# Forming the right operands of a seven-product stage in the tiles of the product before it

## The chip, the cores and the metric

The kernel runs on one core of a Trainium2 chip. The metric is the device time of one execution in microseconds; a comparison is made between medians of several runs. The engines are TensorE (PE; its weight loads are listed as PEld), VectorE (DVE), ScalarE (ACT), GpSimd (POOL) and SyncE (SP), which here only issues DMAs. Times inside an execution are counted from the start of its span.

## What is computed

One transformer-like block over 2048 tokens of width 1024, all in float32: an RMS norm and one input projection, stick-breaking attention (8 heads) beside a gated spatial mixing, an output projection with the residual, and then the part that this change is about:

```
h   = rmsnorm(x, norm_mlp_g)
act = square(relu(h @ w_up))        # 1024 -> 4096
x   = x + act @ w_down              # 4096 -> 1024
out = rmsnorm(x, norm_final_g)
```

## The kernel before, in words

The tokens are worked on in four chunks `c` of 512. Each float32 product is made of three matmuls (`mm3`, L87): an operand is split by `split` (L78) into a high half, which ScalarE rounds (L81), and a low half, which VectorE takes as the difference (L82), and the matmuls are high x high (L89), high x low (L90) and low x high (L91).

The stages that matter stand at the end of the program. Chunks 0 and 1 go through the feed-forward part by plain products: `up_plain` (L592) and `down_plain` (L615). `down_plain` runs over eight groups `g` of the inner width and, in each, over four turns: a chunk (left operand, from `act_d`) times a half of the output columns (right operand, from `w_down`). Chunk and half alternate so that each operand serves two turns, and in the last group the second and the fourth turn also finish a chunk: `finish` (L668) norms each block of 128 rows and stores it through POOL's queue.

Chunks 2 and 3 together go through the feed-forward part by Strassen's method in Winograd's form, with seven products where eight would be needed. `up_seven` (L730) runs over 16 steps `q` of the inner width. In each q it makes seven products of twelve matmuls, in the order 0, 4, 5, 6, 1, 3, 2 (`ORDER`, L417). The right operands, the same for all q, come from the two chunks' `h`: four blocks are loaded from DRAM into tiles `w8` (`Rights`, L675), operand 0 is split at once into its own tiles `x8` (L685), and `rest` (L698) forms the other six as pairs of tiles (high and low) of 8 KB per partition each, and two halves of a subtraction (L703). The left operands are formed per q from a block of `w_up` (`Lefts`, L710) with additions on POOL (L719, L746, L748, L753); their tiles come from the same `w8`. The seven results are combined on VectorE (L770 to L788), squared after relu on ScalarE, and combined once more by `keep_acts` (L579; L582 to L585), which stores seven planes to `s_d` with one DMA per q (L586). `down_seven` (L812) reads these planes back and makes the seven products with `w_down`; its first group needs the tile `new` (L837), which POOL writes (L847).

Tiles come from pools. A pool has so many tiles under a name, and a new tile of that name waits until one is free again, that is until all its users are done, DMAs too. `Room` (L424) holds the names: `t8` are tiles of 8 KB per partition, `t4` of 4 KB. Up to the end of `down_plain` the pool `mp` (L974) has 14 `t8`, two `t4` and the tile `gmlp_t`. Then it is closed (`low.close()`, L1009), and the pool `mlp` (L1012) is laid over its memory, with 12 `t8`, two `acts` of 14 KB and two `t2`. `Rights` and the first `Lefts` are traced before the end of `down_plain` (L1006, L1007), since their tiles lie in the pool `hx` elsewhere, but `rest`, which needs `t8`, is called from within `up_seven` at q = 0 (L736, L751, L756).

The order of each engine's instructions is made by the tile framework when the program is built: it takes them in the order of the source, moved by a model of when each is ready. `together` (L916) interleaves two generators in the source: so many steps of `side` for each step of `main`.

Of the kernel before, what the change touches and what calls it, by code (L numbers as in the profile page):

```python
# [8 lines left out]
F32 = mybir.dt.float32  # L9
F32R = mybir.dt.float32r  # L10
BF16 = mybir.dt.bfloat16
AF = mybir.ActivationFunctionType
ALU = mybir.AluOpType
PSUM = bass.MemoryType.PSUM
DRAM = bass.MemoryType.DRAM

P = 128
D = 1024
# [16 lines left out]
def block_kernel(ctx: ExitStack, tc: tile.TileContext, x, x_t, gmix, w_in, ln_g, ln_b, sgw, sgb,  # L35
# [542 lines left out]

    def keep_acts(q, acts):  # L579

        a11, a12, a21, a22, s1, s2, s4 = (acts[:, i] for i in (0, 1, 6, 3, 4, 5, 2))
        nc.vector.tensor_tensor(s1, a21, a22, ALU.add)  # L582
        nc.vector.tensor_tensor(s2, s1, a11, ALU.subtract)
        nc.vector.tensor_tensor(a21, a11, a21, ALU.subtract)
        nc.vector.tensor_tensor(s4, a12, s2, ALU.subtract)  # L585
        nc.sync.dma_start(s_d[q // 4][:, :, q % 4, :].rearrange("i p t -> p i t"), acts)  # L586

# [26 lines left out]

    def down_plain(rm):  # L615

# [24 lines left out]
        for g in range(ND):  # L641
            lefts, rights = {}, {}
            for turn in range(4):
# [7 lines left out]
                if n not in rights:  # L651
                    rights[n] = right(n, g)
                a, b = lefts[c], rights[n]
                ns = slice(n * 512, (n + 1) * 512)
# [20 lines left out]
    class Rights:  # L675
# [21 lines left out]

        def rest(self, step):  # L698
            if step == 0:
                self.keep(4, self.b11)  # L700
                self.keep(5, self.t2)
                self.keep(1, self.b21)
                self.minus(self.b21, self.b21, self.t2)  # L703
            elif step == 1:
                self.keep(6, self.b12)
            else:
                self.keep(3, self.b21)
                self.keep(2, self.b22)

# [20 lines left out]
    def up_seven(rights, rm, ahead, before_last):  # L730
        hc = rights.hc
        for q in range(16):
            l = ahead if q == 0 else Lefts(rm, q)
            s12, a11, a12, a21, a22, w0, w4 = l.s, l.a11, l.a12, l.a21, l.a22, l.w0, l.w4
            if q == 0:
                rights.rest(0)  # L736

# [11 lines left out]
            w6 = l.operand(a21)  # L749
            if q == 0:  # L750
                rights.rest(1)  # L751
            w1 = l.operand(a12)
            nc.gpsimd.tensor_tensor(a12, a12, s12, ALU.subtract)  # L753
            w3 = l.operand(a22)
            if q == 0:
                rights.rest(2)  # L756
            w2 = l.operand(a12)
            acts = rm.get("acts", [7, TC])
            c11, c21, c22, c12 = acts[:, 0, :], acts[:, 1, :], acts[:, 3, :], acts[:, 6, :]
            u2, u3 = rm.get("t2", [TC]), c22  # L760
            b1 = rm.ps()
# [27 lines left out]
            relu2(c12, c12)  # L789
            keep_acts(q, acts)  # L790
            yield
# [20 lines left out]
    def down_seven(loads, rm):  # L812
# [19 lines left out]
        for g in range(NG):  # L832
# [3 lines left out]
            bs = loads.bs  # L836
            new = rm.get("acts", [2, 2, 512])  # L837

# [15 lines left out]
            for n, i in enumerate(ORDER_D):  # L854
                st = rm.raw8([4, TC])
                nc.sync.dma_start(st, s_d[g][i])
                key = {0: 1, 1: 1, 5: 6, 6: 7, 3: 7, 4: 5, 2: 5}[i]
# [16 lines left out]
                def done(tb):  # L874
# [8 lines left out]
                    elif i == 1:  # L883
                        into(ys[0][tb][:, lo], ps[tb])
                    elif i == 6:
                        into(acc[1][:, tb, :], ps[tb], g == 0)
                    elif i == 4:
                        into(acc[1][:, tb, :], ps[tb])
                        if last_g:
                            plus(ys[1][tb][:, hi], acc[1][:, tb, :])  # L890
                    elif i == 3:
                        into(ys[1][tb][:, lo], ps[tb])
                        if last_g:
                            finish(rm, rm.get("t2", [D], BF16), 3, tb, ys[1][tb], nc.sync)
                    else:
                        into(ys[0][tb][:, hi], ps[tb])
                        if last_g:
                            finish(rm, rm.get("t2", [D], BF16), 2, tb, ys[0][tb], nc.sync)

# [56 lines left out]
    with ExitStack() as es:  # L956
# [15 lines left out]
        gfin_t = gains.tile([P, D], F32, name="gfin_t")  # L972
        low = ExitStack()
        mp = low.enter_context(tc.tile_pool(name="mp", bufs=1, reuse_waits="tile"))  # L974
        gmlp_t = mp.tile([P, D], F32, name="gmlp_t")
        nc.sync.dma_start(gmlp_t, gmlp.broadcast_to([P, D]))
        nc.sync.dma_start(gfin_t, gfin.broadcast_to([P, D]))
        rm = Room(mp, ps_mm, dict(t8=N8, t4=2))
        hTs = []
# [14 lines left out]
        together(o.turn(), side, R_U)  # L994
        down = down_plain(rm)
        assert together(down, side, R_U) is OPEN
    with tc.tile_pool(name="ext", bufs=1, side="right", reuse_waits="tile") as ext, \
# [3 lines left out]
        for part in (o.operands, o.product, o.turn):  # L1001
            together(part(), down, 0.8)
    hx = ctx.enter_context(tc.tile_pool(name="hx", bufs=1, side="right", reuse_waits="tile"))
    rm = Room(None, None, dict(w8=5, raw8=2, x8=2, s12=1, t8=12, acts=2, t2=2),
              dict(w8=hx, raw8=hx, x8=hx, s12=hx))
    rights = Rights(rm)  # L1006
    ahead = Lefts(rm, 0)  # L1007
    together(down)
    low.close()  # L1009
    mm_stack.close()  # L1010
    with tc.tile_pool(name="ps_b", bufs=8, space=PSUM, reuse_waits="tile") as ps_b, \
            tc.tile_pool(name="mlp", bufs=1, reuse_waits="tile") as mlp:  # L1012
        rm.pool, rm.psum = mlp, ps_b
        loads = Down(rm)
        together(up_seven(rights, rm, ahead, lambda: loads.load(0)))
        together(down_seven(loads, rm))
# [38 lines left out]
```

## Time and profile before

| | us |
|---|---|
| median of 3 runs | 2518.61 (2518.34 to 2525.99) |
| the profiled execution's own time | 2518.97 |
| its span | 2517.2 |
| TensorE busy | 2430.1 (97%) |
| VectorE busy | 1694.0 (67%) |
| ScalarE busy | 1145.2 (45%) |
| POOL busy | 309.8 (12%) |

A matmul's record is longer than the distance to the next one, since matmuls are pipelined; what counts is from start to start. In a row of the timeline the bracket tells how long the engine was idle before it, and whom it waited for.

### The profile page before, as it was taken

Reading aid. Unit: us, or ns where it says so; the run is one execution under the profiler, and the core shown is the slowest. Engines: PE = TensorE matmul, PEld = TensorE weight load, DVE = VectorE, ACT = ScalarE, POOL = GpSimd, SP = SyncE. Lnnn points to the kernel's source line nnn. Section 1 sums busy time; section 2 is a strip of 40 time slices with the busy share of each in tenths; the row PEclk is TensorE's granted clock in tenths of the full one; section 3 lists DMA queues with packets and bytes.
Section 4 is the critical chain, followed back from the end, with each engine's and each line's share of the span. In section 5 each row is a group of like instructions: output and inputs, shape, how many; then the busy total and the mean of one; then the engine's idle time right before and its main releaser. Section 6 shows DMA issues by size and latency. Waiting matters only on the chain.

```text
span 2517.2 us, 30341 instructions
## 1 busy us (share of the span) xinstructions
PE 2430.1 (97%) x11424; PEld 1991.5 (79%) x11424; DVE 1694.0 (67%) x2280; ACT 1145.2 (45%) x2004; POOL 309.8 (12%) x255
## 2 busy tenths in 40 slices
PE   8999999997899999999999899999989999999998
PEld 7887788876677888888877688888867888778886
DVE  4643678877767666666668878644667556677788
ACT  5422446445536555555555534322244444433333
POOL 1100011000000000000000000000113322314432
PEclk9999999997999999999989999999999999999999
DMA  9747977679544343433364533343523434753422
GB/s 378 265 141 240 333 260 243 214 211 330 173 164 150 121 126 120 123 115 117 126 255 162 181 130 117 112 182 134 216 85 137 156 141 153 281 218 120 167 101 101
DMA packets 158226, 446.59 MB, mean 177 GB/s; under 512 B 12544, under 2 KB 28928, under 8 KB 138624
## 3 DMA queue, kind: packets, MB, share of 16 engines
q1 hardware_dynamic: 149744, 417.39, 48.5%
q0 software_dynamic: 4032, 25.17, 2.4%
q10 hardware_dynamic: 4304, 2.10, 0.3%
q8 instruction: 90, 1.47, 0.2%
q14 instruction: 56, 0.46, 0.1%
HBM read 314.59 MB, written 130.02 MB: 177 GB/s over the span
## 4 chain that ended last, share of the span: by engine, by line
PE 86%; DVE 8%; issue 3%; DMA 3%; ACT 1%; POOL 0%; POOLq 0%; SPq 0%; DVEq 0%; ACTq 0%
PE mm L91 24%; PE mm L90 24%; PE mm L89 23%; PE tr L370 4%; PE av L389 2%; PE z L346 2%; PE av L388 2%; PE z L345 2%; DVE w L82 2%; DVE t L82 1%; DVE pr L359 1%; PE mm L498 1%; DVE aT L82 1%; PE mm L263 1%; DMA t<-b_d 1%
## 5 line engine op out<-in xcount | busy, mean ns | idle before, releaser
L89 PE MATMUL mm<-t,t 128*128 128x512 f32 x1280 | 503.5, 395 | 0.4 <-DVE t L82 0.4
L91 PE MATMUL mm<-t,t 128*128 128x512 f32 x1280 | 503.5, 393 | 0.0
L90 PE MATMUL mm<-t,t 128*128 128x512 f32 x1280 | 502.3, 393 | 0.0
L359 DVE TENSOR_TENSOR_SCAN pr<-kk,pr,zeros 128x513 f32<-128x513 f32 x192 | 246.3, 1284 | 119.5 <-ACT kk L351 119.0
L351 ACT ACTIVATE kk<-z 128x512 f32<-128x512 f32 (+2 forms) x320 | 172.3, 538 | 296.3 <-PE z L346 158.7
L89 PEld LDWEIGHTS mm<-t,t 128*128 128x128 f32 x1280 | 242.4, 189 | 51.2 <-DVE t L82 0.8
L91 PEld LDWEIGHTS mm<-t,t 128*128 128x128 f32 x1280 | 241.8, 189 | 52.0
L90 PEld LDWEIGHTS mm<-t,t 128*128 128x128 f32 x1280 | 242.1, 189 | 50.0
L81 ACT ACTIVATE aT<-tr 128x512 fp32r<-128x512 f32 (+1 forms) x320 | 173.7, 545 | 107.6 <-PE tr L370 105.9
L82 DVE TENSOR_TENSOR aT<-tr,aT 128x512 fp32r<-128x512 f32 (+1 forms) x320 | 191.1, 598 | 21.6 <-ACT aT L81 21.3
L370 PE MATMUL tr<-ident,b 128*128 128x128 f32 x1088 | 180.9, 279 | 21.9 <-DVE aT L82 17.8
L90 PE MATMUL mm<-w,w 128*128 128x512 f32 x448 | 176.4, 394 | 8.8 <-DVE w L82 8.6
L81 ACT ACTIVATE t<-t 128x1024 fp32r<-128x1024 f32 x104 | 104.7, 1060 | 172.7 <-DMA t<-in_w_down 110.8
L370 PEld LDWEIGHTS tr<-ident,b 128*128 128x128 f32 x1088 | 133.0, 143 | 58.4 <-DVE aT L82 26.6
L91 PE MATMUL mm<-w,w 128*128 128x512 f32 x448 | 175.6, 392 | 0.0
L353 ACT ACTIVATE b<-z 128x512 f32<-128x512 f32 (+2 forms) x320 | 172.1, 539 | 2.6 <-PE tr L370 2.6
L356 DVE TENSOR_TENSOR_SCAN pr<-kk,zeros 128x128 f32<-128x128 f32 (+3 forms) x128 | 104.5, 820 | 96.9 <-ACT kk L351 96.7
L81 ACT ACTIVATE w<-raw 128x512 fp32r<-128x512 f32 (+1 forms) x135 | 106.4, 801 | 132.3 <-PE mm L91 119.9
L91 PE MATMUL mm<-t,w 128*128 128x512 f32 x380 | 150.4, 396 | 2.8 <-DVE w L82 2.8
L82 DVE TENSOR_TENSOR w<-raw,w 128x512 fp32r<-128x512 f32 (+1 forms) x135 | 149.0, 1106 | 3.4 <-ACT w L81 2.9
L90 PE MATMUL mm<-t,w 128*128 128x512 f32 x380 | 149.1, 393 | 1.4 <-DVE t L82 1.4
L82 DVE TENSOR_TENSOR t<-t,t 128x1024 fp32r<-128x1024 f32 x104 | 123.6, 1225 | 39.1 <-ACT t L81 19.4
(214 smaller groups left out, 4765.5 us busy)
## 6 DMA issues: line engine op xcount, KB each, us to landing
w_in<-wi_d SPq DMA_DIRECT2D x40, 1024.0 KB, 8.4
kt<-k_d SPq DMA_DIRECT2D x160, 256.0 KB, 4.9
t<-in_w_down SPq DMA_DIRECT2D x28, 1024.0 KB, 5.1
s_d<-acts SPq DMA_DIRECT2D x16, 1792.0 KB, 6.2
raw<-s_d SPq DMA_DIRECT2D x28, 1024.0 KB, 4.8
t<-wo_d SPq DMA_DIRECT2D x24, 1024.0 KB, 6.9
wi_d<-w_in POOLq DMA_DIRECT2D x20, 1024.0 KB, 9.5
vt<-v_d SPq DMA_DIRECT2D x80, 256.0 KB, 2.7
```

The costliest lines, as they stand in the source:

```text
L81: nc.scalar.activation(hi, src, AF.Copy)
L82: nc.vector.tensor_tensor(lo, src, hi.bitcast(F32), ALU.subtract)
L89: nc.tensor.matmul(ps, lh, rh, start=first, stop=False, skip_group_check=more)
L90: nc.tensor.matmul(ps, lh, rl, start=False, stop=False, skip_group_check=more)
L91: nc.tensor.matmul(ps, ll, rh, start=False, stop=last, skip_group_check=more)
L345: nc.tensor.matmul(z[:, :Z], ql, kt[:, 0, :Z], start=True, stop=False)
L346: nc.tensor.matmul(z[:, :Z], ql, kt[:, 1, :Z], start=False, stop=not diag)
L351: nc.scalar.activation(kk[:, :L], z[:, :L], AF.Sigmoid, scale=-QK_SCALE)
L353: nc.scalar.activation(b[:, :L], z[:, :L], AF.Sigmoid, scale=QK_SCALE)
L356: nc.vector.tensor_tensor_scan(pr[:, L - 1::-1], kk[:, L - 1::-1], zeros[:, :L], 1.0, ALU.mult, ALU.add)
L359: nc.vector.tensor_tensor_scan(pr[:, ::-1], kk[:, ::-1], zeros, carry[tb], ALU.mult, ALU.add)
L370: nc.tensor.transpose(tr[:, tb * P:(tb + 1) * P], bs[tb][:, j * P:(j + 1) * P], ident)
```

## The change

The pool `mp` is not closed any more; it stays to the end and serves the seven-product stages too, with 14 `t8` and three `t4`, one of which first holds `gmlp_t`. `rest` becomes a generator, and it is interleaved with the last two turns of `down_plain`, one step of it for every two steps of the product. The tile `acts` of seven planes is replaced by a `t8` of four planes, a `t4` with s1 and s2, and half of a `t4` with s4, whose other half is u2; so the store of a q becomes three DMAs, and the planes stand in another order in `s_d` (`PLACE`). `new` becomes a `t8`.

```
+    PLACE = (0, 1, 6, 3, 4, 5, 2)
+
+    def keep_acts(q, acts, s12, s4):
+
+        a11, a12, a21, a22 = (acts[:, i] for i in range(4))
+        s1, s2 = s12[:, 0], s12[:, 1]
         nc.vector.tensor_tensor(s1, a21, a22, ALU.add)
         nc.vector.tensor_tensor(s2, s1, a11, ALU.subtract)
         nc.vector.tensor_tensor(a21, a11, a21, ALU.subtract)
         nc.vector.tensor_tensor(s4, a12, s2, ALU.subtract)
-        nc.sync.dma_start(s_d[q // 4][:, :, q % 4, :].rearrange("i p t -> p i t"), acts)
+        dst = s_d[q // 4]
+        nc.sync.dma_start(dst[0:4, :, q % 4, :].rearrange("i p t -> p i t"), acts)
+        nc.sync.dma_start(dst[4:6, :, q % 4, :].rearrange("i p t -> p i t"), s12)
+        nc.sync.dma_start(dst[6, :, q % 4, :], s4)
...
-    def down_plain(rm):
+    def down_plain(rm, placed):
...
+                if g == ND - 1 and turn == 2:
+                    placed.append(True)
...
-        def rest(self, step):
...
+        def rest(self):
+            self.keep(4, self.b11)
+            yield
+            self.keep(5, self.t2)
+            yield
+            self.keep(1, self.b21)
+            yield
+            self.minus(self.b21, self.b21, self.t2)
+            self.keep(6, self.b12)
+            yield
+            self.keep(3, self.b21)
+            yield
+            self.keep(2, self.b22)
...
-            acts = rm.get("acts", [7, TC])
-            c11, c21, c22, c12 = acts[:, 0, :], acts[:, 1, :], acts[:, 3, :], acts[:, 6, :]
-            u2, u3 = rm.get("t2", [TC]), c22
+            acts, both = rm.t8([4, TC]), rm.t4([2, TC])
+
+            c11, c21, c12, c22 = (acts[:, i, :] for i in range(4))
+            u2, u3 = both[:, 0, :], c22
...
-            keep_acts(q, acts)
+            keep_acts(q, acts, rm.t4([2, TC]), both[:, 1, :])
...
-            new = rm.get("acts", [2, 2, 512])
+            new = rm.t8([2, 2, 512])
...
-                nc.sync.dma_start(st, s_d[g][i])
+                nc.sync.dma_start(st, s_d[g][PLACE[i]])
...
-                            finish(rm, rm.get("t2", [D], BF16), 3, tb, ys[1][tb], nc.sync)
+                            finish(rm, rm.t4([D], BF16), 3, tb, ys[1][tb], nc.sync)
...
-        low = ExitStack()
-        mp = low.enter_context(tc.tile_pool(name="mp", bufs=1, reuse_waits="tile"))
-        gmlp_t = mp.tile([P, D], F32, name="gmlp_t")
+        placed = []
+        mp = ctx.enter_context(tc.tile_pool(name="mp", bufs=1, reuse_waits="tile"))
+        rm = Room(mp, ps_mm, dict(t8=N8, t4=3))
+        gmlp_t = rm.t4([D])
...
-    rm = Room(None, None, dict(w8=5, raw8=2, x8=2, s12=1, t8=12, acts=2, t2=2),
-              dict(w8=hx, raw8=hx, x8=hx, s12=hx))
+    rm = Room(mp, ps_mm, dict(w8=5, raw8=2, x8=2, s12=1, t8=N8, t4=3), dict(w8=hx, raw8=hx, x8=hx, s12=hx))
     rights = Rights(rm)
     ahead = Lefts(rm, 0)
-    together(down)
-    low.close()
+    while not placed:
+        next(down)
+    rest = rights.rest()
+    if together(down, rest, 0.5) is OPEN:
+        together(down)
+    for _ in rest:
+        pass
     mm_stack.close()
-    with tc.tile_pool(name="ps_b", bufs=8, space=PSUM, reuse_waits="tile") as ps_b, \
-            tc.tile_pool(name="mlp", bufs=1, reuse_waits="tile") as mlp:
-        rm.pool, rm.psum = mlp, ps_b
+    with tc.tile_pool(name="ps_b", bufs=8, space=PSUM, reuse_waits="tile") as ps_b:
+        rm.psum = ps_b
```

The calls of `rest` inside `up_seven` are gone.

## Rows read from the trace of the kernel before

**Rows 1.** The page's busy time by engine, over the whole span.

```profile
PE 2430.1 (97%) x11424; PEld 1991.5 (79%) x11424; DVE 1694.0 (67%) x2280; ACT 1145.2 (45%) x2004; POOL 309.8 (12%) x255
```

**Rows 2.** TensorE by stretch: length, PE busy (matmuls), granted clock, DMA share, GB/s.

```profile
1780.00:1864.90 84.90, 84.90 (x376) 1.00 0.30 116
1864.90:1925.00 60.10, 49.62 (x195) 0.91 0.35 127
1925.00:2150.00 225.00, 225.00 (x984) 1.00 0.41 150
```

**Rows 3.** TensorE's timeline after the plain down product: start, length, line, matmul, idle before.

```profile
1869.89 0.50 PE L89 MATMUL mm<-t,raw 128*128 128x512 f32 x1 [2.03 <-ACT t L81]
1874.56 0.79 PE L90 MATMUL mm<-t,raw 128*128 128x512 f32 x1 [4.17 <-DVE t L82]
...
1879.42 0.58 PE L89 MATMUL mm<-t,w 128*128 128x512 f32 x1
...
1880.84 0.50 PE L91 MATMUL mm<-t,w 128*128 128x512 f32 x1 [0.37 <-DVE w L82]
...
1884.84 0.50 PE L90 MATMUL mm<-t,w 128*128 128x512 f32 x1 [1.43 <-DVE t L82]
...
1890.58 0.79 PE L91 MATMUL mm<-t,w 128*128 128x512 f32 x1 [2.48 <-DVE w L82]
...
1893.62 0.40 PE L89 MATMUL mm<-t,w 128*128 128x512 f32 x1
```

**Rows 4.** ScalarE's, VectorE's and POOL's timelines around the end of the plain down product.

```profile
1868.78 2.01 ACT L81 ACTIVATE t<-w 128x1024 fp32r<-128x1024 f32 x2 [1.68 <-DMA out_y<-t]
...
1868.64 1.28 DVE L672 SCALAR_TENSOR_TENSOR t<-t,nf_r,gfin_t 128x1024 f32<-128x1024 f32 x1 [1.36 <-POOL nf_r L75]
1873.28 6.90 DVE L82 TENSOR_TENSOR t<-w,t 128x1024 fp32r<-128x1024 f32 x6 [3.35 <-DMA out_y<-t]
...
1848.55 0.57 POOL L673 DMA_DIRECT2D out_y<-t  x1 [1.62 <-DVE t L672]
```

**Rows 5.** A stretch near that end: length, then PE, PEld, DVE, ACT, POOL busy.

```profile
1846.00:1865.00 19.00, 19.00 (x86) 15.73 (x85) 9.02 (x13) 3.45 (x6) 3.50 (x7) 1.00 0.20 84
```

**Rows 6.** SyncE's and VectorE's timelines in the first three q.

```profile
1879.65 25.83 SPq L716 DMA_DIRECT2D raw<-in_w_up  x3
1910.93 0.37 SPq L586 DMA_DIRECT2D s_d<-acts  x1
...
1924.73 1.03 DVE L582 TENSOR_TENSOR acts<-acts 128x512 f32<-128x512 f32 x1 [0.89 <-ACT acts L590]
...
1938.39 0.69 DVE L782 TENSOR_TENSOR acts<-mm,t 128x512 f32<-128x512 f32 x1 [4.68 <-PE mm L91]
```

**Rows 7.** DMA issues: queue, count, KB each, median us from issue to landing.

```profile
s_d<-acts SPq DMA_DIRECT2D x16, 1792.0 KB, 6.2
...
raw<-in_w_up SPq DMA_DIRECT2D x16, 1024.0 KB, 4.8
...
b_d<-u SPq DMA_DIRECT2D x16, 256.0 KB, 4.0
...
out_y<-t POOLq DMA_DIRECT2D x8, 512.0 KB, 2.9
```

**Rows 8.** Timelines where the down stage begins; last, the landing of L586's store at 2178.

```profile
2206.01 0.79 PE L90 MATMUL mm<-w,w 128*128 128x512 f32 x1 [5.34 <-DVE w L82]
...
2193.89 2.57 DVE L582 TENSOR_TENSOR acts<-acts 128x512 f32<-128x512 f32 x1 [0.23 <-ACT acts L590]
...
2204.74 1.21 DVE L82 TENSOR_TENSOR w<-acts,w 128x1024 fp32r<-128x1024 f32 x1
...
2192.61 3.30 POOL L847 TENSOR_TENSOR acts<-t,t 128x1024 f32<-128x1024 f32 x1 [1.77 <-issue]
...
2178.14 1.16 SPq L586 DMA_DIRECT2D s_d<-acts  x1
...
DMA to landing us min/median/max: 14.4/14.4/14.4
```

More of the change, by code (lines that the diff above doesn't have):

```diff
@@ L576, in turn @@
                     nc.sync.dma_start(h_d[self.c - 2][kk], self.hT[kk])
-    def keep_acts(q, acts):
-        a11, a12, a21, a22, s1, s2, s4 = (acts[:, i] for i in (0, 1, 6, 3, 4, 5, 2))
+    PLACE = (0, 1, 6, 3, 4, 5, 2)
+    def keep_acts(q, acts, s12, s4):
+        a11, a12, a21, a22 = (acts[:, i] for i in range(4))
+        s1, s2 = s12[:, 0], s12[:, 1]
         nc.vector.tensor_tensor(s1, a21, a22, ALU.add)
@@ L696, in keep @@
             split4(t, src)
-        def rest(self, step):
[L699 to L708, printed above, removed]
+        def rest(self):
[11 more added lines that the diff above has]
+            self.keep(2, self.b22)
     class Lefts:
@@ L734, in up_seven @@
             s12, a11, a12, a21, a22, w0, w4 = l.s, l.a11, l.a12, l.a21, l.a22, l.w0, l.w4
-            if q == 0:
-                rights.rest(0)
             def form(w, i, ps, first):
@@ L749, in up_seven @@
             w6 = l.operand(a21)
-            if q == 0:
-                rights.rest(1)
             w1 = l.operand(a12)
@@ L754, in up_seven @@
             w3 = l.operand(a22)
-            if q == 0:
-                rights.rest(2)
             w2 = l.operand(a12)
-            acts = rm.get("acts", [7, TC])
-            c11, c21, c22, c12 = acts[:, 0, :], acts[:, 1, :], acts[:, 3, :], acts[:, 6, :]
-            u2, u3 = rm.get("t2", [TC]), c22
+            acts, both = rm.t8([4, TC]), rm.t4([2, TC])
+            c11, c21, c12, c22 = (acts[:, i, :] for i in range(4))
+            u2, u3 = both[:, 0, :], c22
             b1 = rm.ps()
@@ L897, in done @@
                         if last_g:
-                            finish(rm, rm.get("t2", [D], BF16), 2, tb, ys[0][tb], nc.sync)
+                            finish(rm, rm.t4([D], BF16), 2, tb, ys[0][tb], nc.sync)
                 if last_g and n >= 5:
@@ L972, in block_kernel @@
         gfin_t = gains.tile([P, D], F32, name="gfin_t")
-        low = ExitStack()
-        mp = low.enter_context(tc.tile_pool(name="mp", bufs=1, reuse_waits="tile"))
-        gmlp_t = mp.tile([P, D], F32, name="gmlp_t")
+        placed = []
+        mp = ctx.enter_context(tc.tile_pool(name="mp", bufs=1, reuse_waits="tile"))
+        rm = Room(mp, ps_mm, dict(t8=N8, t4=3))
+        gmlp_t = rm.t4([D])
         nc.sync.dma_start(gmlp_t, gmlp.broadcast_to([P, D]))
         nc.sync.dma_start(gfin_t, gfin.broadcast_to([P, D]))
-        rm = Room(mp, ps_mm, dict(t8=N8, t4=2))
         hTs = []
@@ L994, in block_kernel @@
         together(o.turn(), side, R_U)
-        down = down_plain(rm)
+        down = down_plain(rm, placed)
         assert together(down, side, R_U) is OPEN
```

## The prediction

> **What bounds the kernel now.** I read the busy shares first: TensorE is busy 97% of the span and VectorE, next, 67% [rows 1], so time can only be won where TensorE is not fed at full speed. The busy time by stretch shows where that is [rows 2]. From 1780 to 1864.9 us, the end of the plain down product, TensorE has no idle time at a granted clock of 1.00. From 1864.9 to 1925, the first q of the seven-product stage, it is busy 49.6 of 60.1 us and the mean clock is 0.91. From 1925 to 2150 it is full again: 984 matmuls in 225 us, one per 0.2287 us.
>
> TensorE's timeline of the first dip names the waits [rows 3]. The twelve matmuls of product 0 follow the plain down product without a pause, since its right operand lies in its own tiles. Then TensorE waits 2.03 us for ScalarE's high half of right operand 4, 4.17 us for VectorE's low half, and 0.37, 1.43 and 2.48 us for further halves: 10.48 us. After two of these waits the matmuls start 0.43 us apart, the lower of the clock's two levels: 12 starts from 1874.56 to 1879.42 (11 intervals, 4.86 us where 11 x 0.2287 = 2.52 would do) and 8 from 1890.58 to 1893.62 (7 intervals, 3.04 instead of 1.60). That is 2.34 + 1.44 = 3.78 us more.
>
> The ScalarE, VectorE and POOL timelines say why the halves are late [rows 4]. The first ScalarE split of operand 4 waits for the landing of an output row block and starts at 1868.78; six VectorE splits (6.90 us, 1.15 us each) start at 1873.28, after waiting for the last of those blocks. The pool for these operands lies over the old pool's memory, so its tiles come free only as the plain product's last rows leave.
>
> **The change part by part.** *Right operands in the old pool's tiles.* The six operand pairs (4, 5, 1, 6, 3, 2) take 12 of the 14 tiles of the pool that now stays open. During the last two turns of the plain product (third and fourth of g = 7) ten are held: 4 by the results, 2 by the left pair, 4 by the two right pairs. So four are free by the start of the third turn, which holds operands 4 and 5. Two more come when chunk 0's results have left: its last store is issued at 1848.55 and such a store takes 2.9 us [rows 4, 7], so by about 1851.5 there is room for operand 1. The third turn's right pair comes free when that turn ends, one turn (48 matmuls, about 11 us) before 1864.9, so near 1854: operand 6. The rest come free at 1864.9: operands 3 and 2. Products run in the order 0, 4, 5, 6, 1, 3, 2, each 12 x 0.2287 = 2.74 us, so counted from 1864.9 operand 4 is due at +2.7, 5 at +5.5, 6 at +8.2, 1 at +11.0, 3 at +13.7 and 2 at +16.5. Every operand has room 10 us before it is due, and one takes 2 x 1.15 = 2.3 us of VectorE.
>
> *Does VectorE have that time?* From 1846 to 1865 it is busy 9.0 of 19 us [rows 5]. Eight splits (operands 4, 5, 1, 6) and the two halves of the subtraction of b21, which have the same shape, add 10 x 1.15 = 11.5 us: 20.5 in 19, so about 1.5 us runs over, if operand 4 isn't already made earlier. After 1864.9 come that 1.5, operands 3 and 2 (4.6), the last results (2 x 1.28 [rows 4] and a bank reading of 0.69 [rows 6], 3.3 in all), five left splits of the shape of such a reading (3.4) and three to four readings of product banks (2.5): 15.3 us before operand 2 is due at +16.5. It fits, narrowly. I take 0.9 us for what is late anyway, between 0 and the 5 us of the second rival.
>
> *Left operands of q = 0 and 1.* They use tiles that hold the right blocks until those are split; with the splits done earlier these come free earlier, and the load for q = 1, issued at 1879.65 [rows 6], moves forward. It lands in 4.8 us [rows 7] and is due at +19.2. Nothing new waits here, and ScalarE, with half of VectorE's load [rows 5], covers its share.
>
> *What is saved.* Lower bound: the listed waits and slow matmuls, 10.48 + 3.78 = 14.3 us. Upper bound: 60.1 us less the 195 recorded matmuls at full pitch, 60.1 - 195 x 0.2287 = 15.5 us (a missing record would make this too large). I take the middle, 14.9. What is won stays won, because the next 225 us are bound by TensorE alone [rows 2].
>
> *The store in three parts.* One store of 1792 KB per q becomes 1024, 512 and 256 KB: 32 more issues on SyncE, 0.37 us each, 0.74 us per q of 19.2 us [rows 6]. The next load stands behind them; it is wanted a whole q later, so this costs nothing. The bytes and rows are the same, and the planes are only renumbered for the later reads.
>
> *The small tiles.* u2 and s4 share one of three 4 KB tiles and s1, s2 take another, two per q. So s1 of one q, VectorE's first addition at L582, now needs a tile from the q before, once its store has landed. The store of q = 0 is issued at 1910.93 and lands in 6.2 us; the next L582 is at 1924.73, so there are 7.6 us to spare [rows 6, 7]. If this cover went, VectorE would stop there, and behind it the readings of the product banks on which TensorE depends.
>
> *Where the down stage begins.* TensorE waits 5.34 us at 2206.01 for a low half that VectorE makes at 2204.74, behind four additions L582 to L585 which began at 2193.89 and take 2.57 us and more instead of the 1.03 at 1924.73, beside POOL [rows 6, 8]. With about 2.3 us of slow matmuls behind it (taken as long as the longer one above) this place costs 7.7. Two parts of the change touch it. The tile `new` came from the two `acts` buffers, and POOL's first write to it at 2192.61 falls on the landing of q = 14's store (2178.14 + 14.4 = 2192.5); taken from the common pool it need not wait, and POOL is done sooner: up to 7.7 gained. Against that, L582 of q = 15 now needs that store landed, with 1.4 us to spare: a landing 4 us later costs about 3. I take 0 between -7.7 and +3. By the Trainium skill, DMA: Bandwidth & Descriptors, "Anatomy of one DMA — SWDGE (gpsimd) path", a DMA carries about 2 us whatever its size (stated for another issuing path than this one); two more per q would by that estimate land the last part 4 us later, L582 would be 2.6 us late, and the sum here would be +2.6. The rows speak for less: a 256 KB store lands in 4.0 us, a 1792 KB one in 6.2 [rows 7], so a part issued 0.74 us later should land about that much later.
>
> Sum, against the profiled execution's own 2518.97 us (span 2517.2; the median of the runs is 0.36 lower): 2518.97 - 14.9 + 0.9 + 0 = 2505.0 us.
>
> **The rivals.** *A second gain.* The wait at 2206 goes too: 2505.0 - 7.7 = 2497.3, with parts of it 2498 to 2502. For it: `new` is the write that waited. Against: VectorE's four additions have the earlier place in its order whatever POOL does.
>
> *VectorE becomes the bound for a q.* The margin above is 1 us. If splits stand in front of the readings of the product banks, or POOL's left-operand work (four operations of about 1.6 us, half the shape of the one of 3.30 us) slows them as at 2193.89 [rows 8], some 5 us of TensorE's wait come back, with one stretch of slow matmuls (1.9, the mean of the two): 2505.0 + 6.9 = about 2512. By the Trainium skill, SBUF — State Buffer, "Who interferes with whom", a VectorE instruction with two SBUF inputs and a POOL one that reads SBUF block each other in full; by that estimate four POOL operations of 1.6 us would add 6.4 us to VectorE here, and the time would be this rival's. The rows at 2193.89 agree with the rule.
>
> *The change doesn't do what it says.* The splits are traced earlier, but are placed behind the results' last work, or get the tiles that come free last: 2518.97 less at most 3, 2516 to 2519. For it: an order written by a planner isn't seen in the source. Against: product 0's operand, formed in free tiles, was ready when its product began [rows 3].
>
> *Slower: the 4 KB tiles.* If every q's L582 waited for the landing, VectorE's stop would reach TensorE once the landing outlasts the 13.8 us between store and next L582 and VectorE's longest idle time in a q, 4.7 us [rows 6]: from 18.5 us on, each further us costs 15. At 20 us that is 22.5 us, 2527.5 in all. Against: 6.2 us as a median, 14.4 at worst [rows 7, 8].
>
> **How the numbers follow.** About 0.3%, 7.6 us, is what a measurement of this kernel can tell from no change: faster is below 2511.0. Forecast 0.58 (2502 to 2508), second gain 0.11, VectorE the bound 0.13 (2508 to 2515, half of it still faster), no effect 0.12, slower 0.06. Faster: 0.58 + 0.11 + 0.07 = 0.76; same: 0.06 + 0.12 = 0.18; slower 0.06. The range of 2498 to 2514 leaves out the last two cases and the ends of the others.
>
> **What would show it.** Right: splits of operands 4, 5, 1 and 6 before the last matmul of the plain product; no TensorE idle time over 1 us and a clock of 1.00 in the 60 us after it; the load for q = 1 before that product's end; three stores per q without a longer L582. Wrong: a TensorE wait on a right operand's half after product 0 (the no-effect case, or VectorE's), L582 waiting on a DMA (the 4 KB tiles), or a longer wait than 5.34 us where the down stage begins.

## The result and the profile after

The changed kernel takes 2506.59 us (median of 5 runs, 2500.51 to 2508.97) against 2520.29 (5 runs, 2518.34 to 2525.99) in the same set: a ratio of 0.9937, 95% interval 0.9917 to 0.9957. It is faster by 0.6%, 13.7 us; 2505.0 was predicted.

Which part moved is read from TensorE's timeline. The first matmul of product 0 (`mm<-x,raw`) and the first of the down stage (`mm<-w,w`) cut the span in three. In the kernel before they are these:

```profile
1864.96 0.39 PE L89 MATMUL mm<-x,raw 128*128 128x512 f32 x1
...
2188.69 0.39 PE L89 MATMUL mm<-w,w 128*128 128x512 f32 x1
```

In the changed kernel, where the second waits a little, with the longest wait that TensorE has behind it:

```profile
1867.56 0.39 PE L89 MATMUL mm<-x,raw 128*128 128x512 f32 x1
...
2176.72 1.19 PE L89 MATMUL mm<-w,w 128*128 128x512 f32 x4 [0.88 <-ACT w L81]
...
2189.79 0.80 PE L90 MATMUL mm<-w,w 128*128 128x512 f32 x1 [6.08 <-DVE w L82]
```

So, in the profiled executions (the last column is the span less the second start):

| profile of | up to product 0 | seven-product up stage | down stage to the end |
|---|---|---|---|
| before (span 2517.2) | 1865.0 | 323.7 | 328.5 |
| after (span 2507.2) | 1867.6 | 309.2 | 330.5 |
| difference | +2.6 | -14.6 | +2.0 |

The profile page's busy time hardly moved [rows 1]: TensorE does the same work, and it loses less between.

```profile
PE 2431.0 (97%) x11424; PEld 1992.6 (79%) x11424; DVE 1699.1 (68%) x2280; ACT 1146.0 (46%) x2004; POOL 311.2 (12%) x255
```

TensorE by stretch (length, busy time and matmuls, granted clock, DMA share, GB/s), which answers to [rows 2]; the second stretch is the first 60.1 us from product 0:

```profile
1780.00:1867.60 87.60, 87.60 (x388) 1.00 0.31 118
1867.60:1927.70 60.10, 60.10 (x264) 1.00 0.46 167
1927.70:2150.00 222.30, 222.30 (x971) 1.00 0.43 156
```

The dip is gone: 264 matmuls where 195 stood, no idle time, clock 1.00 instead of 0.91. VectorE's timeline shows why; in a row, `t<-w` is a split of a right operand, L681 an output row block's norm:

```profile
1833.09 2.35 DVE L82 TENSOR_TENSOR t<-w,t 128x1024 fp32r<-128x1024 f32 x2
...
1849.03 1.22 DVE L82 TENSOR_TENSOR t<-w,t 128x1024 fp32r<-128x1024 f32 x1
...
1856.54 2.36 DVE L82 TENSOR_TENSOR t<-w,t 128x1024 fp32r<-128x1024 f32 x2 [1.86 <-PE mm L90]
...
1860.55 2.35 DVE L82 TENSOR_TENSOR t<-w,t 128x1024 fp32r<-128x1024 f32 x2
...
1871.42 2.35 DVE L82 TENSOR_TENSOR t<-w,t 128x1024 fp32r<-128x1024 f32 x2
...
1874.95 2.35 DVE L82 TENSOR_TENSOR t<-w,t 128x1024 fp32r<-128x1024 f32 x2
1877.22 1.27 DVE L681 SCALAR_TENSOR_TENSOR t<-t,nf_r,gfin_t 128x1024 f32<-128x1024 f32 x1
```

The six pairs of halves are made in the source's order, 4, 5, 1, 6, 3, 2, where the products run 4, 5, 6, 1, 3, 2, and each is made before its product begins: operand 4 at 1833, 34 us before product 0; 5 at 1846.7 and 1849.0; 1 and 6 before 1863; 3 and 2 at 1871 to 1877, while the first products run. Before, six such splits stood in one block from 1873.28 [rows 4]. The last norm now comes after the splits, at 1877.22, and TensorE doesn't wait for it.

SyncE's timeline, at the start of the up stage and where the down stage's loads begin (L592, L591 and L593 are the three stores of a q: s1 and s2, the four planes, s4):

```profile
1871.53 18.77 SPq L727 DMA_DIRECT2D raw<-in_w_up  x3
1895.37 0.37 SPq L592 DMA_DIRECT2D s_d<-t  x1
...
1897.18 1.57 SPq L593 DMA_DIRECT2D s_d<-t  x1
...
2162.88 0.36 SPq L592 DMA_DIRECT2D s_d<-t  x1
2163.52 0.36 SPq L591 DMA_DIRECT2D s_d<-t  x1
2164.08 0.94 SPq L593 DMA_DIRECT2D s_d<-t  x1
2165.12 5.58 SPq L813 DMA_DIRECT2D t<-in_w_down  x4
```

In q = 14 the three stores now go out ahead of the four loads that the down stage begins with. The first of these is issued 11.6 us before the stage's first matmul (2176.72 - 2165.12); before it was 13.8, three of the loads stood ahead of the store at 2178.14 [rows 8], and POOL, which starts on them, began 3.3 us ahead of that matmul (2188.69 - 2185.42). SyncE's and POOL's rows in the kernel before:

```profile
2174.92 3.11 SPq L807 DMA_DIRECT2D t<-in_w_down  x3
...
2185.42 2.94 POOL L846 TENSOR_TENSOR t<-t,t 128x1024 f32<-128x1024 f32 x1 [21.22 <-DMA t<-in_w_down]
```

VectorE's and POOL's timelines there in the changed kernel, which answer to [rows 8]:

```profile
2180.02 2.44 DVE L586 TENSOR_TENSOR t<-t 128x512 f32<-128x512 f32 x1 [0.36 <-ACT t L597]
2182.49 2.75 DVE L587 TENSOR_TENSOR t<-t,t 128x512 f32<-128x512 f32 x1
2185.16 2.83 DVE L588 TENSOR_TENSOR t<-t 128x512 f32<-128x512 f32 x1
2187.92 0.68 DVE L589 TENSOR_TENSOR t<-t,t 128x512 f32<-128x512 f32 x1
2188.52 1.21 DVE L82 TENSOR_TENSOR w<-t,w 128x1024 fp32r<-128x1024 f32 x1
...
2178.45 3.46 POOL L852 TENSOR_TENSOR t<-t,t 128x1024 f32<-128x1024 f32 x1 [27.27 <-DMA t<-in_w_down]
2181.99 2.70 POOL L853 TENSOR_TENSOR t<-t,t 128x1024 f32<-128x1024 f32 x1
2184.65 2.79 POOL L854 TENSOR_TENSOR t<-t 128x1024 f32<-128x1024 f32 x1
```

POOL does write `new` (L853) without waiting for any store, but it starts late, 1.7 us behind the stage's first matmul, since the load that it needs landed late, and runs beside the same four additions. Three of them are slow instead of four, and the low half behind them (2188.52) is still what TensorE waits 6.08 us for, where it waited 5.34.

### The profile page after: what moved, and what is told of

The parts are those of the page before. It is cut to its first block, busy times and chain, and to the rows that moved or that the text cites. A ratio compares the mean times of both kernels' runs of the same rounds, so it can differ in the third digit from the quotient of the medians.

```text
span 2507.2 us, 30443 instructions
## 1 busy us (share of the span) xinstructions
PE 2431.0 (97%) x11424; PEld 1992.6 (79%) x11424; DVE 1699.1 (68%) x2280; ACT 1146.0 (46%) x2004; POOL 311.2 (12%) x255
## 4 chain that ended last, share of the span: by engine, by line
PE 87%; DVE 6%; DMA 4%; issue 1%; ACT 1%; SPq 0%; POOL 0%; POOLq 0%; DVEq 0%; ACTq 0%
PE mm L90 24%; PE mm L91 24%; PE mm L89 24%; PE tr L370 4%; PE av L389 2%; PE av L388 2%; PE z L346 2%; PE z L345 2%; DVE w L82 2%; DMA v_d<-qkv_st 1%; DVE pr L359 1%; PE mm L498 1%; DVE t L82 1%; PE mm L263 1%; DMA t<-b_d 1%
```

## The experiments

The time up to product 0 differs from one profiled execution to the next by far more than the other two parts, so each kernel below is read by its parts as well as by its time. The profiles of all runs, with the parts worked out as above:

| kernel | up to product 0 | up stage | down stage |
|---|---|---|---|
| e0_after (the changed kernel) | 1863.2 | 309.1 | 330.4 |
| e1_late | 1861.8 | 308.8 | 330.6 |
| e6_behind | 1869.1 | 323.5 | 331.8 |
| e2_split | 1869.4 | 323.7 | 323.0 |
| e7_two | 1872.1 | 308.6 | 330.8 |
| e8_hold | 1867.5 | 321.5 | 330.6 |
| e3_loads, e9_loads2 | 1861.5, 1865.0 | 308.1, 308.1 | 326.8, 326.8 |
| e4_sums, e10_sums2 | 1864.2, 1860.2 | 309.0, 309.1 | 325.9, 327.4 |
| e5_both, e11_both2 | 1857.7, 1868.9 | 308.1, 308.1 | 322.4, 324.0 |

**The changed kernel once more,** beside others on the same chip.

> The changed kernel once more, as the measure for the three kernels beside it and for how much its runs differ: 2500 to 2509, with waits where the down stage begins of about 9 us in three places.

It took 2503.53 us (6 runs; 2520.71 for the kernel before, 11 runs), ratio 0.9941 [0.9926, 0.9957]. Its up and down stage are the first profile's within 0.1 us, and its waits where the down stage begins are 0.86, 6.09 and 2.15 us, the 9 us in three places that were expected.

**The pool alone, without the interleaving in the source.** The question is whether the gain comes from the tiles that stay open or from the place in the source where the operands are formed.

```
-    while not placed:
-        next(down)
-    rest = rights.rest()
-    if together(down, rest, 0.5) is OPEN:
...
+    together(down)
```

with the calls of `rest` put back into `up_seven` at q = 0, where they stood in the kernel before.

> The pool stays open as in the change, but the six operand pairs are traced where they were before, inside the seven-product stage at q = 0, and not between the steps of the plain product. Theory (tiles): what was won comes from the tiles that are free while the plain product still runs; the place in the source does not matter, since the planner moves work to where it is ready. Then TensorE has no wait over 1 us in the 60 us behind the plain product, the granted clock there is 1.00, and the time is that of the changed kernel, about 2506 (ratio to before 0.993 to 0.996). Rival (order): the interleaving did it; then the waits of before return, some 10 us and a clock near 0.91 in that stretch, and the time is 2517 to 2521.

It took 2504.19 us (6 runs; 2518.96 for the kernel before, 23 runs), ratio 0.9939 [0.9924, 0.9953], like the changed kernel. VectorE's rows in the 54 us around product 0 are the same as the changed kernel's, operation by operation. TensorE in the 60.1 us from product 0, by stretch:

```profile
1861.80:1921.90 60.10, 60.10 (x263) 1.00 0.46 167
```

So the pool that stays open, with its tiles, is the whole gain of the up stage (308.8 us here), and the interleaving adds nothing: the framework's order puts the splits into the same places, wherever the source has them.

**The pool open, the splits held back.** Here the tiles are as in the changed kernel, but the splits of the six pairs are queued behind the last norm of the results on ScalarE and VectorE.

```
-    if together(down, rest, 0.5) is OPEN:
-        together(down)
+    together(down)
+    with tc.issue_after(last[0].ins), tc.issue_after(last[1].ins):
+        for _ in rights.rest():
+            pass
```

(`last` holds the last square and the last norm of `finish`, L679 and L681 in the changed kernel.)

> The pool stays open, but every split of the six operand pairs is queued on ScalarE and VectorE behind the last norm of the plain product's results. It parts two things that the kernel before had together: splits that come late, and tiles that are not free until the results have left. Theory: lateness alone brings most of it back, because VectorE then makes six operands of 2.3 us each one behind the other while TensorE takes 2.74 us per product: TensorE's waits after product 0 are 6 to 10 us in all with one or two stretches at the lower clock, and the time is 2512 to 2518. Rival (landing): what cost the time before was mainly the wait for the output rows to land; with tiles free, the waits are under 4 us and the time is under 2511.

It took 2521.93 us (12 runs), ratio 1.0010 [1.0000, 1.0021]: nothing is left of the gain. TensorE by stretch, from its product 0:

```profile
1869.10:1929.10 60.00, 50.82 (x198) 0.91 0.35 127
```

TensorE's and VectorE's timelines in that stretch:

```profile
1875.25 0.51 PE L90 MATMUL mm<-t,raw 128*128 128x512 f32 x1 [2.52 <-DVE t L82]
...
1879.86 0.50 PE L89 MATMUL mm<-t,w 128*128 128x512 f32 x1 [1.79 <-ACT w L81]
...
1896.91 0.50 PE L89 MATMUL mm<-t,w 128*128 128x512 f32 x1 [1.98 <-DVE t L782]
...
1873.98 9.16 DVE L82 TENSOR_TENSOR t<-w,t 128x1024 fp32r<-128x1024 f32 x8
```

Eight splits stand in one block from 1873.98 to 1883.1, right behind the norm and without a wait for a DMA. The waits after product 0 sum to 9.2 us (0.24, 2.52, 1.79, 1.01, 0.94, 0.70, 1.98), with the clock at 0.91, and the up stage is 323.5 us, as before (323.7). This is within the waits expected and 4 us above the time expected. What follows: it is enough that the splits come behind the results' last work. How much the landing of those rows [rows 4] added in the kernel before is not shown: there the block of splits starts 8.3 us after product 0 and here 4.9, and the up stage comes out the same.

**The three stores alone.** The kernel before with its own pool and its `acts` of seven planes, but stored by three DMAs in the new order of planes.

```
-        nc.sync.dma_start(s_d[q // 4][:, :, q % 4, :].rearrange("i p t -> p i t"), acts)
+        dst = s_d[q // 4]
+        nc.sync.dma_start(dst[0:4, :, q % 4, :].rearrange("i p t -> p i t"), acts[:, 0:4])
+        nc.sync.dma_start(dst[4:6, :, q % 4, :].rearrange("i p t -> p i t"), acts[:, 4:6])
+        nc.sync.dma_start(dst[6, :, q % 4, :], acts[:, 6])
```

> The kernel before, with one part of the change alone: the store of each q in three parts of 1024, 512 and 256 KB, planes renumbered; pools and order of the operands as before. Theory: nobody waits for a part, so the waits behind the plain product are those of before (about 10 us) and the time is within 3 us of before, 2517 to 2523. Rival: the parts carry a fixed cost each and crowd the loads where the down stage begins; then the wait of 5.34 us there grows by 2 to 4 us, and the time is 2522 to 2526.

It took 2514.05 us (12 runs), ratio 0.9976 [0.9966, 0.9985]: a small gain, which neither the theory (2517 to 2523) nor the rival had, by the profile all of it in the down stage (323.0 us; before 328.5), with the up stage as before (323.7). VectorE's and POOL's timelines at the start of that stage:

```profile
2195.40 0.69 DVE L584 TENSOR_TENSOR acts<-acts 128x512 f32<-128x512 f32 x1 [1.36 <-ACT acts L595]
...
2197.34 0.69 DVE L587 TENSOR_TENSOR acts<-acts 128x512 f32<-128x512 f32 x1
2197.94 3.40 DVE L82 TENSOR_TENSOR w<-t,w 128x1024 fp32r<-128x1024 f32 x1
...
2193.05 2.40 POOL L853 TENSOR_TENSOR t<-t 128x1024 f32<-128x1024 f32 x1
2197.60 2.66 POOL L852 TENSOR_TENSOR acts<-t,t 128x1024 f32<-128x1024 f32 x1 [2.15 <-DMA s_d<-acts]
```

POOL stood idle from 2195.45 to 2197.60, waiting for the store of q = 14 before it could write `new`, and the four additions fell into that gap: 0.69 us each. The split that follows, beside POOL again, takes 3.40. In the kernel before the same additions took 2.57 us and more [rows 8]. So the store in three parts is not costly in itself; it moves the order, and the wait that POOL had for `new` was useful to VectorE.

**The small tiles.** The third 4 KB tile was to be held through the up stage. The first try took it with two writes by POOL, one at the start and one meant for the end:

```
+        hold = rm.t4([2, TC])
+        nc.gpsimd.memset(hold[:, 0, 0:1], 0.0)
...
+        nc.gpsimd.memset(hold[:, 0, 0:1], 0.0)
```

> The changed kernel with one of the three 4 KB tiles held through the whole up stage, so that two are left for u2 with s4 and for s1 with s2. Theory (the third tile is the cover of the new wait): u2 of the next q must then wait for the landing of this q's store, some 9 us after TensorE is done with its product; ScalarE stands, and TensorE loses 5 to 10 us in each of 15 q: 2580 to 2650. Rival (the wait is covered anyway by the idle time of VectorE and ScalarE): under 2515.

One run: 2513.2 us, with an up stage of 308.6 us. The second write had no input, so the framework put it right behind the first, at 1873.3 us, and the tile was free again. This run tells nothing of the tiles. In the second try the last use reads data of q = 15:

```
+                nc.gpsimd.tensor_tensor(hold[:, 0, :], hold[:, 0, :], c11, ALU.add)
```

> The changed kernel with one of its three 4 KB tiles truly held: POOL fills it once before q = 0 and uses it again only in q = 15, behind the last square of that q. (In the earlier try the second use ran right after the first, so nothing was held.) Two tiles are left for two requests per q, so u2 of each q needs a tile that was stored at the end of the q before. Theory (the third tile and the q between a store and the next L582 are what hides the stores): a store is issued at the end of a q and lands in 5 to 6 us, u2 is wanted 2.7 us after the q's begin, and ScalarE, which makes u2, stands in front of its splits; so each of 15 q waits 2 to 5 us, and with the half-rate matmuls after a wait that is 40 to 100 us more: 2545 to 2610. Rival (the stores are hidden whatever the number of tiles, and the cover was never needed): 2500 to 2512, no more waits than the changed kernel.

One run: 2521.27 us, with an up stage of 321.5, 12.4 us more than the changed kernel's, well below the 40 us of the theory and above the rival. What ScalarE waited for from 1880 to 2192 us (in all, times, longest), and TensorE by stretch:

```profile
ACT t L771 <- DMA s_d<-t: 30.4, 13, 5.6
```

```profile
1867.50:1930.00 62.50, 62.50 (x274) 1.00 0.50 177
...
2070.00:2130.00 60.00, 60.00 (x263) 1.00 0.43 145
2130.00:2189.00 59.00, 49.50 (x200) 0.91 0.61 208
```

Between the stretches shown TensorE is busy without a gap as well (307 matmuls in each 70 us). TensorE's and SyncE's timelines in the last of these:

```profile
2161.68 0.50 PE L89 MATMUL mm<-t,w 128*128 128x512 f32 x1 [2.38 <-ACT t L771]
...
2179.01 0.80 PE L89 MATMUL mm<-t,w 128*128 128x512 f32 x1 [7.13 <-ACT t L771]
...
2150.84 0.94 SPq L816 DMA_DIRECT2D x<-in_w_down  x2
2152.72 0.37 SPq L592 DMA_DIRECT2D s_d<-t  x1
...
2175.42 0.37 SPq L592 DMA_DIRECT2D s_d<-t  x1
```

ScalarE (L771, u2) did wait for a store in 13 of the q, some 2.3 us each, and in eleven of them TensorE lost nothing: it goes on in the other PSUM banks until ScalarE has read the one that it needs again (product 0 of q = 15 starts at 2148.11, before ScalarE reads that of q = 14 at 2161.03). Only in q = 14 and 15 does the wait come through, 2.38 and 7.13 us. The store that u2 of q = 14 waits for, at 2152.72, stands right behind two loads for the down stage and lands in 8.2 us, where 2.8 is the median. The one that u2 of q = 15 waits for, at 2175.42, lands in 2.8 us; but it is issued 3.9 us after TensorE's last matmul of q = 14, and no further q is there for TensorE to go on with. In this one execution the third tile is worth 12.4 us, all of it there.

**The down stage's begin: the order of stores and loads.** This undoes one thing that the change brought along: the stores of q = 14 are issued behind the first four loads.

```
                 before_last()
+                with tc.issue_after(ins):
+                    stores(14, *late["14"])
```

(`ins` is the last of these loads, and the stores of q = 14 are left out at their old place.)

> The changed kernel, with the three stores of q = 14 issued behind the first four loads for the down stage and not ahead of them. Theory (two causes in a row: late loads, then VectorE's four additions of q = 15 ahead of the split that TensorE waits for): the first load lands 2 to 5 us earlier and the small wait of 0.9 us at the start of the down stage goes, but the low half that TensorE waits for still stands behind the additions, so the wait of 6.1 us shrinks by 2 us at most; time 0 to 4 us below the changed kernel. Rival (the loads alone): with POOL's work earlier the whole 9 us goes, and the time falls by 8 to 10 us.

It took 2497.62 us (6 runs; 2520.71 for the kernel before, 11 runs), ratio 0.9921 [0.9904, 0.9939]. A second set of runs:

> The kernel with q = 14's three stores issued behind the first four loads for the down stage, once more, to have it beside its two neighbours in one set of runs: ratio to the kernel before near 0.992 (0.9905 to 0.9935); its profile's time from the first matmul of the down stage to the end near 326.8, against 330.4 of the changed kernel, if the gain is that of the order and not of one execution.

2500.10 us (6 runs; 2519.56 for the kernel before, 11 runs), ratio 0.9928 [0.9913, 0.9943], and again a down stage of 326.8 us against 330.4 and 330.5. SyncE's and TensorE's timelines (first set):

```profile
2155.84 3.96 SPq L828 DMA_DIRECT2D t<-in_w_down  x4
2159.90 2.86 SPq L597 DMA_DIRECT2D s_d<-t  x1
...
2191.33 0.50 PE L90 MATMUL mm<-w,w 128*128 128x512 f32 x1 [2.98 <-DVE w L82]
```

and VectorE's first addition of q = 15 in the same run (L590 here):

```profile
2186.06 1.69 DVE L590 TENSOR_TENSOR t<-t 128x512 f32<-128x512 f32 x1
```

The first load is issued 13.8 us before the stage's first matmul (at 2169.6), as in the kernel before. TensorE doesn't wait at that matmul any more, and the longest wait is 2.98 us instead of 6.08. That is more than the theory's 2 us off that wait and less than the rival's whole of it, and so is the time, 5.9 us below the changed kernel's 2503.53 of the same set. Part by part this kernel has 1.0 us less of the up stage and 3.6 of the down stage. The edit moved more than the DMAs, though: with the loads earlier the framework also moved the four additions of q = 15 behind more of the splits, from 3.3 us after the stage's first matmul (2180.02) to 16.5 (2186.06). So how much of the 3.6 us is the loads' alone is not shown.

**The additions of q = 15 later.** The four additions L586 to L589 of the last q are queued behind the splits of the second down product:

```
+                if g == 0 and i == 5:
+                    with tc.issue_after(made[0].ins):
+                        keep_acts(15, *late["15"])
```

> The changed kernel, with the four additions of q = 15 queued on VectorE behind the splits of the second product of the down stage. Theory: the split for which TensorE waits 6.1 us then starts when POOL and ScalarE are done with its source, about 2.5 to 3 us earlier; 3 to 4 us of the wait stay, because the loads land as late as before; time 2 to 5 us below the changed kernel. Rival (the additions alone): the wait goes whole, 7 to 9 us below. Other rival: the additions, later, stand in front of the next splits beside POOL, and the wait only moves: no gain.

It took 2505.50 us (6 runs), ratio 0.9949 [0.9933, 0.9966], no better than the changed kernel (0.9941), though its profiled down stage was 4.5 us shorter. A second set of runs:

> The kernel with the four additions of q = 15 queued behind the splits of the second down product, once more, since its profile's down stage was 4.5 us shorter than the changed kernel's and its time was not. If the down stage is really shorter and the first set met a longer part before product 0, this one's ratio comes out at 0.991 to 0.993 and its profile has again 325 to 327 us from the first down matmul to the end. If the profile's one execution was an exception, the ratio stays at 0.994 to 0.996 and the profile has 329 to 331.

2498.44 us (6 runs), ratio 0.9924 [0.9909, 0.9939], with a down stage of 327.4 us. The two sets differ by more than the additions can be worth; the shorter down stage came back, 3.0 to 4.5 us. In place of the 6.08 us, TensorE's longest wait in the first 25 us of the stage is 1.80 and 1.77 us in the two profiles, though the loads stand behind the stores as in the changed kernel. (A wait of 2.15 us, 30 us into the stage, stands in both; the kernel before and the changed one have it too, 33 us into theirs.) That the first set met a longer time before product 0 is likely and not shown, since only one execution of each set has a trace.

**Both together.** The edits of the last two kernels in one.

> Both of the edits before: the stores of q = 14 behind the loads, and the additions of q = 15 behind the splits of the second product. Theory (both causes in a row): the wait where the down stage begins is under 2 us in all and the clock stays at 1.00; time 7 to 10 us below the changed kernel, about 2497. Rival: another wait takes their place (the third product's left operand, whose plane is read back from DRAM behind the loads), and the time is within 4 us of the changed kernel.

2497.90 us (6 runs), ratio 0.9914 [0.9898, 0.9931], 5.6 us below the changed kernel of the same set, where 7 to 10 were expected. A second set of runs:

> Both moves of the down stage's begin together, once more. If the two add up, 3.5 us below the kernel with the loads alone (ratio 0.990 or less) and a down stage of 322 to 323 us; if the additions' move brings nothing beside the loads', the same ratio as the kernel with the loads alone within 0.001.

2496.72 us (5 runs), ratio 0.9920 [0.9905, 0.9936]. By the profiles the two add up: 322.4 and 324.0 us of down stage, 6.5 to 8.1 below the changed kernel's, with one wait over 1 us left in the first 25 us of that stage, here in TensorE's timeline of the second set:

```profile
2184.57 0.50 PE L90 MATMUL mm<-w,w 128*128 128x512 f32 x1 [1.04 <-DVE w L82]
```

By the times, 0.9914 and 0.9920 against 0.9921 and 0.9928 for the loads alone, the intervals overlap, and by the measure that was set for the second set (0.990 or less) the second edit brings nothing. The kernel is faster than the kernel before. Against the changed kernel the ratio intervals just touch (up to 0.9931, from 0.9926), but in the first set all six runs (2489.88 to 2499.55) lie below all six of the changed kernel (2500.69 to 2506.94). That its second edit helps beside the first is shown by the stage, in two profiles, and not by the time.

## Why the prediction was right

**Right operands in the old pool's tiles.** The sum took 14.9 us off, between 14.3 and 15.5, and gave 0.9 back; the up stage became 14.6 us shorter, so 0.3 us came back on the middle value. The mechanism is shown from both sides: the open pool without the interleaving brings all of it, and with the pool open and the splits late all of it is lost. The price of lateness read from the waits and half-rate starts [rows 3] held: the second of these kernels lost 14.3 us (323.5 - 309.2).

**The tiles' due times.** Operand 4 was made at 1833.1, 34 us before product 0, earlier than needed; the rest come in the order 5, 1, 6, 3, 2, with 1 ahead of 6, which is the source's order and the one in which the step had counted free tiles. The step on VectorE's time said that it fits with 1 us to spare. It was easier: the last half of operand 2 was done at 1877.3 and due at 1867.6 + 16.5 = 1884.1, 6.8 us to spare, because operand 4 and half of operand 5 were made ahead of the last 19 us, and the results' last norm gave way. The rival "VectorE becomes the bound" is wrong by that margin.

**The rival "the change doesn't do what it says"** was given for the order of a planner that the source doesn't show. That half of it is true: the interleaving moves nothing. The rest falls: with the tiles free the same planner put the splits early, wherever the source had them.

**The load for q = 1** was to be issued before the end of the plain product. It came 4.0 us after it (1871.53 against 1867.56), where before it was 14.7 us after (1879.65 against 1864.96) [rows 6]. The sum doesn't rest on it, since the load is not what TensorE waits for. (ScalarE's "half of VectorE's load" in that step is 3.45 against 9.02 us [rows 5], less than half; that errs to the safe side.)

**The store in three and the small tiles** cost nothing in the up stage, as said. L586 waited in 15 of the 16 q, for ScalarE alone and 0.4 us at most, and no store held it up. (It took 1.52 us in most q where L582 had taken 1.04; "without a longer L582" was among the signs of being right and came true for the wait, not for the addition itself. TensorE had no wait from it.) In q = 0 to 13 the parts landed in 2.8 us (512 KB), 4.9 (1024 KB) and 4.7 (256 KB) as medians. The held tile shows, in one execution, that the cover was larger than the step had it: without the third tile the stop is ScalarE's, not VectorE's, and eleven of thirteen such stops are absorbed. The rival "Slower: the 4 KB tiles" needed landings over 18.5 us; the longest of a part stored in the up stage was 8.4, in q = 14.

**Where the down stage begins** was taken at 0 between -7.7 and +3, and it was +2.0: inside the bounds, and the step whose reasons held least. One of the signs set for being wrong came here: the longest wait grew from 5.34 to 6.08 us. The step looked for a gain from `new`, which POOL would write earlier. POOL did not wait for a store, but the load that it starts from came late: the changed order puts 1.79 MB of stores ahead of the four loads, which are issued 11.6 us instead of 13.8 before the stage. The kernel with the loads first is 3.6 us shorter in that stage; since the additions moved in it as well, the late loads are a likely cause of the +2.0 and not a proven one. The rival "A second gain" fell by what was said against it: the four additions kept their place ahead of the split (2180.02 to 2188.5), and with them moved away alone, the loads as late as before, the stage is 3.0 to 4.5 us shorter. And a POOL that waits is no loss there: in the kernel with the three stores alone its wait of 2.15 us left VectorE four additions at 0.69 us.

By the Trainium skill, DMA: Bandwidth & Descriptors, "Anatomy of one DMA — SWDGE (gpsimd) path", a DMA has a fixed cost of about 2 us, stated for DMAs that GpSimd issues; the estimate from it was +2.6 us here, near the +2.0 measured, by a late L586. The trace doesn't bear that cause out: L586 at 2180.02 waited 0.36 us, for ScalarE, and the last part of q = 14, issued at 2164.08, landed in 8.4 us, at 2172.5, 7.5 us ahead of it.

**The sum of the parts.** In the profiled executions -14.6 and +2.0 make -12.6 us, and the time before product 0 added 2.6 by itself. In the medians it is -13.7, where -14.0 was forecast; that these two are so near is in part luck, since the parts that the change touches gave 1.4 us less than forecast. TensorE's instructions up to product 0 are the same in the same order in both kernels; still this part took from 1857.7 to 1872.1 us over the profiles, while two profiles of the same kernel differ by 0.1 at most in the up stage and 1.6 in the down stage. So most of the spread between these executions lies ahead of what was changed. Why it varies was not tried.

## What to carry to other kernels

When two stages share memory, keep one pool open over the border and let the next stage's operands take the tiles as they come free: here a pool that was closed and laid over made its first tiles wait for the last rows of the old one, and with the pool open the place in the source changed nothing. When a store is split or a tile is moved to another pool, look at what else in the queue changes its place: here stores slid ahead of the next stage's loads, and putting them back, with what else moved by it, was worth 3.6 us of that stage. And ask of every wait that is taken from an engine which neighbour was fast because of it.

## What the runs showed of the hardware

**VectorE beside POOL.** The same addition of two 128x512 planes took 0.69 us where POOL waited (2195.40 in the kernel with three stores) and 2.44 to 2.83 us beside POOL's additions (2180.02 to 2185.16 in the changed kernel); a 128x1024 split took 1.21 and 3.40. By the Trainium skill, SBUF — State Buffer, "Who interferes with whom", the port pair that VectorE and POOL share is an exclusive lock. The trace agrees. It shows the price here: the three slow additions together are 6.0 us above 3 x 0.69. That TensorE's wait behind them is 6.08 us is not the same figure over again: with the additions moved away, 1.80 us of that wait are left.

**A small store behind larger ones.** Of the three stores of a q the one of 512 KB, issued first, landed in 2.8 us (median of q = 0 to 13), the one of 1024 KB behind it in 4.9, and the one of 256 KB, issued 1.8 us after the first, in 4.7. So the last part lands about 6.5 us after the first was issued, much like the one store of 1792 KB with its 6.2 us [rows 7]: splitting the store did not add up the times of its parts. That a part's time follows from the bytes ahead of it more than from its own is likely and not shown, since another 256 KB store, b_d, takes 4.0 us as well [rows 7].
